# One copy of each RWKV chunk step to ScalarE, rope work held out of the lead-in, four affine values to VectorE

## The chip, the core and the metric

The kernel runs on one core of one Trainium2 chip. The engines are TensorE (PE in the profile, PEld for its weight loads), VectorE (DVE), ScalarE (ACT), GpSimd (POOL) and SyncE (SP), which here only issues DMAs. The metric is device time of one launch in microseconds, the median of several runs. Before the change it is 2287.57 us (three runs, 2287.49 to 2290.06).

## What is computed

Two layers of a hybrid decoder trunk over 1024 tokens of width 1024, then an RMSNorm. Cut to what matters here:

```python
mod = c_act @ w_ada + b_ada                      # shift, scale, gate
h = rms_norm(x, norm_g) * (1.0 + scale) + shift  # the affine values
proj = h @ w_in                                  # one wide projection
# three mixers on parts of proj: pooling, retention (rotary on q and k), RWKV-7
def step(S, inp):                                # RWKV-7, per head of 64
    r_t, w_t, k_t, v_t, a_t, b_t = inp
    sa = jnp.einsum('bhvk,bhk->bhv', S, a_t)
    S = (S * w_t[:, :, None, :] + sa[..., None] * b_t[:, :, None, :]
         + v_t[..., None] * k_t[:, :, None, :])
    return S, jnp.einsum('bhvk,bhk->bhv', S, r_t)
y = jnp.einsum('btnw,nwd->btnd', branches, w_branch)
merged = jnp.sum(sigmoid(gate_logits) * y, axis=2)
x = x + gate * (merged @ w_out)
```

## The kernel before

**How the order comes about.** The program is first recorded as a list of operations (class `Log`, from line 205), each with the operations it has to wait for, kept in `o.after`: value 1 means "after its end", value 2 "after its start". Then `plan` (line 334) replays the list with a cost model of each engine: at each step it takes the engine that can start soonest and gives it the ready operation with the smallest key. Only then are the instructions emitted, in that order, and each engine runs its own list strictly in order. All instructions are issued from line 540, so groups of the profile are told apart by the names of their tiles. A subtraction on GpSimd in some lanes may be planned on VectorE instead (`flex`). Because the plan is greedy and one list, an operation added or moved at one place shifts the order of nearly everything behind it.

**Number format of the big matmuls.** Every wide operand is split in a high and a low part, `hhi` and `hlo` for the activations, `wh` and `wl` (or `wbig`) for weights, and each product is the sum of three matmuls, hi by hi, lo by hi and hi by lo. The splits are a cast on ScalarE and a subtraction on GpSimd or VectorE.

**The lead-in** (`lead_in`, line 1810) is the first 70 or so microseconds. It loads x in two halves of 512 tokens (h) of eight tiles (kt), forms the RMSNorm, and forms shift and scale from `w_ada` in six groups: `coef(0)` to `coef(5)`; groups 4 and 5 give the coefficients of tiles 4, 5 and of tiles 6, 7. Each group, except group 1, is a chain of eight VectorE multiply-adds into `ada_ps`, the last into `ada_acc`, then tiny matmuls that sum over partitions (`sums`), then `mod` and `acoef` on VectorE (`ada_end`, line 736). Then `one(h, kt)` (line 1848) runs `affine` (line 1770): two ScalarE activations of the same values, one into `hhi`, one back into `x`; `low` subtracts to get `hlo`; `mms` multiplies with the first three weight items. `acc6` holds their six accumulators (`acc`, `ch`, `two`).

**Other work that the plan puts into the lead-in.** `setup_rest` (line 661) copies the constant `bone` and derives vectors of layer 1 (`omu`, `vec`) on VectorE. `rope_tables` (line 757), in lane "mix", makes sine and cosine for the retention's rotary, in two halves, from tiles `posi`, `ang`, `nrot`, `over`. They are recorded after the lead-in, but their inputs are there early, and `plan` places them where an engine is free in its model.

**The chunk step** (`rwkv_task`, lines 1514 to 1563). After preparation, each layer has four pairs of heads, each with 16 chunks of 64 tokens: 128 steps in all, each dependent on the one before. A step is: matmul `two<-S,AR`; VectorE adds to `xst`; two small matmuls `ch<-xst,G`, which solve the rows; a copy of the solved rows into `Z[0:64, c]` (line 1538, on VectorE); matmul `ch<-Z,BKt`; VectorE forms the next state `S`. Beside it ScalarE scales the state (`SP`) and copies the output (`y<-two`). TensorE fills the waits of a step with the big matmuls of projection items, as far as the plan foresees the waits; it leaves an estimated 300 ns of slack behind an operand from another engine.

**What follows.** Gates that are left, Strassen-like products of pairs of items (`forms`), the branch projections and the output projection, all big matmuls; and then the second layer.

Of the kernel before, what the change touches and what calls it, by code (L numbers as in the profile page):

```python
# [204 lines left out]
class Log:  # L205


    def __init__(self, nc, tc):
        self.nc, self.tc = nc, tc
        self.on = False  # L210
        self.ops = []
        self.tag = {}
        self.acc = {}
        self.lane = ""
        self.group = None
        self.real = {"DVE": nc.vector, "POOL": nc.gpsimd}
        self.vector = Proxy(self, "DVE", nc.vector)
        self.scalar = Proxy(self, "ACT", nc.scalar)
        self.gpsimd = Proxy(self, "POOL", nc.gpsimd)
        self.tensor = Proxy(self, "PE", nc.tensor)  # L220
        self.sync = Proxy(self, "SP", nc.sync)

    def call(self, eng, name, real, a, k):
        is_ap = lambda x: hasattr(x, "tensor") and hasattr(x, "ap")
        aps = [x for x in a if is_ap(x)] + [v for q, v in k.items() if q != "out" and is_ap(v)]
        if "out" in k:
            outs, ins = [k["out"]], aps
        else:
            outs, ins = aps[:1], aps[1:]
        o = self.group if self.on else None  # L230
        if isinstance(o, Op):
            o.calls.append((real, a, k, name))
            o.outs += outs
            o.ins_ += ins
        else:
            o = Op()
            o.eng, o.calls, o.outs, o.ins_ = eng, [(real, a, k, name)], list(outs), list(ins)
            o.lane, o.n, o.late, o.inst = self.lane, name, not self.on, None
            o.no_dep = o.own_dep = o.behind = None
            o.held = False  # L240
            o.flex = self.on and FLEX and eng == "POOL" and name == "tensor_tensor" and self.lane in FREE and k.get("op") != ALU.pow
            o.after, o.allocs, o.took = {}, [], []
            o.idx = len(self.ops)
            self.ops.append(o)
            if self.on and self.group is not None:
                self.group = o
        reads = ins + (outs if name == "matmul" and k.get("start") is False else [])
        for x, w in [(x, False) for x in reads] + [(x, True) for x in outs]:
            if x.space == DRAM and x.tensor.name.startswith(("in_", "out_t")):
                continue  # L250
            r = pieces(x)
            old = self.acc.setdefault(x.tensor.name, [])
            keep = []
            for p, pw, pr in old:
                if (w or pw) and p is not o and meet(r, pr):
                    o.after[p] = max(o.after.get(p, 0), 1)
                    if w and covers(r, pr):
                        continue
                keep.append((p, pw, pr))
            keep.append((o, w, r))  # L260
            self.acc[x.tensor.name] = keep
        if not self.on:
            o.inst = real(*a, **k)
        return o
# [289 lines left out]
def trunk_kernel(ctx, tc, xT, cvec, pos, vecs, consts, w_ada, w_all, pool_w, lora_w, out):  # L554
# [448 lines left out]
    def wprep(big=False):  # L1003
        if wready and wready[-1][0][0] == "forms":
            return
        for l, it in planner:
            if it[0] not in ("merge", "idle", "forms"):
                break
            wready.append((it, None))
            if it[0] != "merge":  # L1010
                return
        else:
            return
        t = None
        if it[0] == "out" and it[1] >= 2 and kept(l):
            if it[2]:
                wready.append((it, keep_w[it[1]]))
                return
            if it[1] < 6:
                t = r8("wout")  # L1020
            else:
                if it[1] == 6:
                    keep_w["G"] = gtile("wG")
                t = keep_w["G"][:, 2048 * (it[1] - 6) : 2048 * (it[1] - 5)]
        elif big:
            t = r8("wbig")
        parts = []
        for j in range(2):
            if t is not None:
                o = j * D  # L1030
                hi, lo = t[:, o : o + HF].bitcast(F32R), t[:, o + HF : o + D].bitcast(F32R)
            else:
                hi = wp.tile([P, HF], F32R, tag="wh", name=nm("wh"), bufs=3)
                lo = wp.tile([P, HF], F32R, tag="wl", name=nm("wl"), bufs=3)
            raw = wp.tile([P, HF], F32, tag="wr", name=nm("wr"), bufs=3)
            nc.sync.dma_start(out=raw, in_=w_all[l, ITEMS.index(it[:2] if it[0] == "out" else it), j])
            split(raw, hi, lo)
            parts.append((hi, lo))
        if it[0] == "out":
            keep_w[it[1]] = parts  # L1040
        wready.append((it, parts))
# [243 lines left out]
    def rwkv_task(l, hp, kT, rT, vp, lt, lw):  # L1285
# [228 lines left out]
        for c in range(16):  # L1514
            par = c % 2
            prog[(l, hp)] = c
            if c % 8 == 0:
                y = t_ri("y")
            S, Sn = SS[par], SS[1 - par]
            pcc = pc[:, c : c + 1]  # L1520
            SP = sb.tile([P, P], F32, tag="SP", name=nm("SP"), bufs=1)
            nc.scalar.activation(SP, S, AF.Copy, scale=pcc)
            cy = cyt()
            sa = mmul(cy[:, 0:P], jt(AR, slice(0, P), c), S)
            if c:
                sa.no_dep = yout[-1]
                sa.after[yout[-1]] = 2
            if c > 1:
                sa.own_dep = yout[-2]
            nc.vector.tensor_tensor(xst[0:64, :], cy[64:128, 0:P], AV[:, c * P : (c + 1) * P], op=ALU.add)  # L1530
            yield wait(xst)
            ch = ps_c.tile([P, HF], F32, tag="ch", name=nm("ch"))
            for hd in range(2):
                cols = slice(64 * hd, 64 * hd + 64)
                u0 = (16 * hd + c) * P
                n = min(65, 32 * P - u0 - 64)
                mmul(ch[0:n, cols], Gf[:, u0 + 64 : u0 + 64 + n], xst[:, cols])
            nc.vector.tensor_copy(Z[0:64, c, :], ch[0:64, 0:P])
            yield wait(Z)
            mmul(ch[:, P : 2 * P], BKt[:, c, :], Z[:, c, :])  # L1540
            for hd in range(2):
                rw = slice(64 * hd, 64 * hd + 64)
                nc.vector.scalar_tensor_tensor(
                    Sn[rw, rw], ch[rw, P + 64 * hd : P + 64 * hd + 64], pc[rw, c : c + 1], SP[rw, rw],
                    op0=ALU.mult, op1=ALU.add,
                )
            yield 500
            for hd in range(2):
                cols = slice(64 * hd, 64 * hd + 64)
                mmul(  # L1550
                    cy[0:65, cols],
                    G[:, 16 * hd + c, 0:65],
                    Z[:, c, cols],
                    start=False,
                    skip_group_check=True,
                )
            o = (c % 8) // 2 * P
            yout.append(nc.scalar.copy(y[64 * par : 64 * par + 64, o : o + P], cy[0:64, 0:P]).ins)
            yield wait(Sn)
            if c % 8 == 7:  # L1560
                h = c // 8
                yn = layer_norm(y, 8, 64, RWKV_EPS, t_ri, nc.gpsimd)
                posts[l, hp, h] = add("post", rwkv_post(l, hp, h, yn, bvs[h]))
# [206 lines left out]
    def affine(h, kt):  # L1770
        x = xin[h][kt]
        b, a = mod[0][:, SHIFT[kt] : SHIFT[kt] + 1], acoef[0][:, kt : kt + 1]
        hi, lo = hb("hhi"), hb("hlo")
        nc.scalar.activation(hi, x, AF.Identity, bias=b, scale=a)
        nc.scalar.activation(x, x, AF.Identity, bias=b, scale=a)
        h_cur[h].append((hi, lo))

    def low(eng, h, kt):
# [27 lines left out]
    def steps(g, n):  # L1806
        for _ in range(n):
            next(g)

    def lead_in():  # L1810
        V, G_ = nc.vector, nc.gpsimd
# [30 lines left out]
        def coef(g):  # L1842
            if g in COLUMNS:
                ada_columns(g)
            else:
                steps(gs[g], 9)

        def one(h, kt):
            normed(h, kt)
            affine(h, kt)  # L1850
            low(G_, h, kt)
            mms(h, kt)
# [33 lines left out]
        one(1, 3)  # L1886
        one(0, 5)
        coef(5)
        one(1, 4)
        one(0, 6)  # L1890
        one(1, 5)
# [15 lines left out]
    for i in range(3):  # L1907
        evac(FIRST[i], acc6[1][i], 1)
    wprep()
    setup_rest()  # L1910
    add("mix", rope_tables())
    late_ada = [(0, g) for g in (6, 7)] + [(1, g) for g in range(8)]

    for l in range(L):
# [468 lines left out]
```

## Time and profile before

| what | value |
|---|---|
| median of three runs | 2287.57 us |
| the profiled execution | 2284.81 us |
| its span | 2282.9 us |
| mean granted TensorE clock | 0.996 |
| VectorE busy | 1627.5 us (71%) |
| ScalarE busy | 907.4 us (40%) |
| GpSimd busy | 623.8 us (27%) |

Busy time is the sum of an engine's instructions. For TensorE it is rough: matmuls are pipelined, their ends are modelled, and a 128x512 one is shown as some 400 ns though the next starts some 230 ns later. A stall shorter than that difference does not show as idle time of PE; it does show before the weight load (PEld). "Who waited for whom" counts idle time of an engine before an instruction and names the operation that ended it.

### The profile page before, as it was taken

The page shows a single profiled execution, that of the slowest core. Times are in us where ns is not written, and L with a number is a line of the kernel's source. Part 1 is how long each engine was busy: PE and PEld are TensorE (multiplying, and loading weights), DVE is VectorE, ACT ScalarE, POOL GpSimd, SP SyncE. Part 2 cuts the span into 40 slices and gives each one's busy share as a digit, 9 for nine tenths or more (in the row PEclk, how much of TensorE's full clock was granted, in tenths as well). Part 3 has the DMA queues.
Part 4 walks back from the last instruction along what each step waited for, and adds up shares of the span by engine and source line. Part 5 has one row for each costly group of instructions (what it writes and reads, how often), then busy time and mean ns, then how long its engine had stood idle before and what let it go on. Part 6 is the DMA issues. An engine that isn't in the chain of part 4 may idle for free.

```text
span 2282.9 us, 35125 instructions
## 1 busy us (share of the span) xinstructions
PE 2246.9 (98%) x13076; PEld 1866.6 (82%) x13076; DVE 1627.5 (71%) x2907; ACT 907.4 (40%) x1671; POOL 623.8 (27%) x545
## 2 busy tenths in 40 slices
PE   7999999999999999999999999999999999999998
PEld 6788888888888888888888888888888888888888
DVE  7997876878888644667677778688785844465854
ACT  5734433434235344323454344243332444442243
POOL 2223323323325201331122232332432500041211
PEclk9999999999999999999999999999999999999999
DMA  8212111112356633664541111111122633256442
GB/s 317 81 49 67 33 44 47 44 50 76 117 165 210 213 126 97 226 191 164 170 131 34 41 33 39 56 39 47 51 71 75 194 116 111 88 171 225 133 131 84
DMA packets 138043, 248.86 MB, mean 109 GB/s; under 512 B 15632, under 2 KB 18960, under 8 KB 137872
## 3 DMA queue, kind: packets, MB, share of 16 engines
q1 hardware_dynamic: 137872, 246.61, 33.9%
q8 instruction: 103, 1.69, 0.3%
q14 instruction: 68, 0.56, 0.1%
HBM read 187.04 MB, written 59.51 MB: 108 GB/s over the span
## 4 chain that ended last, share of the span: by engine, by line
PE 89%; DVE 8%; issue 1%; ACT 1%; DMA 0%; POOL 0%; SPq 0%; DVEq 0%; POOLq 0%; ACTq 0%
PE acc L540 73%; PE two L540 3%; PE ch L540 3%; PE av L540 1%; PE ro L540 1%; PE g L540 1%; DVE two L540 1%; DVE tm L540 1%; DVE ksq L540 1%; PE lw L540 1%; PE m L540 1%; PE rkv L540 1%; PE bt L540 1%; DVE G L540 1%; PE rs L540 0%
## 5 line engine op out<-in xcount | busy, mean ns | idle before, releaser
L540 PE MATMUL acc<-hhi,wh 128*128 128x512 f32 x1488 | 599.3, 403 | 0.6 <-DVE vp L540 0.6
L540 PE MATMUL acc<-hlo,wh 128*128 128x512 f32 x1488 | 598.5, 402 | 0.0
L540 PE MATMUL acc<-hhi,wl 128*128 128x512 f32 x1488 | 595.9, 401 | 0.0
L540 POOL TENSOR_TENSOR wl<-wr,wh 128x512 fp32r<-128x512 f32 x175 | 237.9, 1361 | 582.2 <-ACT wh L540 485.3
L540 PEld LDWEIGHTS acc<-hhi,wh 128*128 128x128 f32 x1488 | 280.6, 189 | 51.2 <-issue 1.5
L540 PEld LDWEIGHTS acc<-hhi,wl 128*128 128x128 f32 x1488 | 280.7, 189 | 49.2 <-issue 0.7
L540 PEld LDWEIGHTS acc<-hlo,wh 128*128 128x128 f32 x1488 | 280.8, 189 | 48.6 <-issue 0.7
L540 ACT CAST wh<-wr 128x512 fp32r<-128x512 f32 x242 | 149.1, 617 | 292.8 <-PE acc L540 230.0
L540 PE MATMUL acc<-T,wh 128*128 128x512 f32 x576 | 177.5, 390 | 0.0
L540 PEld LDWEIGHTS acc<-T,wh 128*128 128x128 f32 x576 | 108.2, 188 | 22.4
L540 DVE TENSOR_TENSOR wl<-wsum,wh 128x512 fp32r<-128x512 f32 x75 | 53.5, 713 | 94.8 <-ACT wh L540 94.4
L540 ACT COPY y<-two 64x128 f32<-64x128 f32 x128 | 32.9, 257 | 211.7 <-PE two L540 208.2
L540 PE MATMUL acc<-T,wl 128*128 128x512 f32 x288 | 112.3, 390 | 0.0
L540 DVE SCALAR_TENSOR_TENSOR S<-ch,pc,SP 64x64 f32<-64x64 f32 x256 | 71.9, 281 | 54.8 <-PE ch L540 46.8
L540 POOL TENSOR_TENSOR oz<-ol,oz 128x512 fp32r<-128x512 f32 x10 | 14.3, 1435 | 327.9 <-DVE wl L540 259.2
L540 ACT CAST wh<-wsum 128x512 fp32r<-128x512 f32 x96 | 59.5, 620 | 95.8 <-PE acc L540 93.7
L540 DVE TENSOR_TENSOR xst<-two,MT 64x128 f32<-64x128 f32 x128 | 37.5, 293 | 68.9 <-PE two L540 44.9
L540 DVE TENSOR_TENSOR two<-two,tm 64x30 f32<-64x30 f32 (+14 forms) x240 | 78.8, 328 | 7.0
L540 DVE TENSOR_TENSOR tm<-MT,two 64x30 f32<-64x30 f32 (+14 forms) x240 | 76.3, 318 | 8.2 <-ACT two L540 1.3
L540 DVE TENSOR_TENSOR wl<-wraw,wh 128x512 fp32r<-128x512 f32 x53 | 37.6, 710 | 61.5 <-ACT wh L540 61.5
L540 PE MATMUL acc<-oy,wh 128*128 128x512 f32 x256 | 80.0, 394 | 0.0
L540 PE MATMUL acc<-oG,wh 128*128 128x512 f32 x256 | 79.0, 390 | 0.0
(328 smaller groups left out, 4899.6 us busy)
## 6 DMA issues: line engine op xcount, KB each, us to landing
wr<-in_w_all SPq DMA_DIRECT2D x268, 256.0 KB, 2.7
wraw<-in_w_all SPq DMA_DIRECT2D x96, 256.0 KB, 2.7
gd<-gsg SPq DMA_DIRECT2D x96, 256.0 KB, 2.0
gs<-gd SPq DMA_DIRECT2D x96, 256.0 KB, 3.8
wada<-in_w_ada SPq DMA_DIRECT2D x80, 256.0 KB, 3.1
ol<-od SPq DMA_DIRECT2D x48, 256.0 KB, 3.4
traw<-hd SPq DMA_DIRECT2D x32, 256.0 KB, 3.0
x<-in_xT SPq DMA_DIRECT2D x16, 256.0 KB, 5.1
```

Of the source, the lines that this page charges most:

```text
L540: o.inst = f(*a, **k)
```

## The change

Three edits. The copy of the solved rows in each chunk step goes from VectorE to ScalarE. Operations of `setup_rest` and `rope_tables` on VectorE, ScalarE and GpSimd get an added order, "not before the start of" the last operation of `coef(5)`; their DMAs, on SP, do not. And for tiles 6 and 7 the affine value that goes back into `x` is computed on VectorE; `hhi` stays on ScalarE.

```diff
@@ class Log
+        self.quiet = None
...
+            if self.quiet is not None and eng in ("DVE", "ACT", "POOL"):
+                o.after[self.quiet] = 2
@@ rwkv_task
-            nc.vector.tensor_copy(Z[0:64, c, :], ch[0:64, 0:P])
+            nc.scalar.copy(Z[0:64, c, :], ch[0:64, 0:P])
@@ affine
         nc.scalar.activation(hi, x, AF.Identity, bias=b, scale=a)
-        nc.scalar.activation(x, x, AF.Identity, bias=b, scale=a)
+        if kt < 6:
+            nc.scalar.activation(x, x, AF.Identity, bias=b, scale=a)
+        else:
+            nc.vector.tensor_scalar(x, x, a, b, op0=ALU.mult, op1=ALU.add)
@@ before lead_in
+    coefs = []
+
+    def quietly(gen):
+        while True:
+            nc.quiet = coefs[0]
+            dt = next(gen, None)
+            nc.quiet = None
+            if dt is None:
+                return
+            yield dt
@@ lead_in
         coef(5)
+        coefs.append(nc.ops[-1])
@@ after lead_in
+    nc.quiet = coefs[0]
     setup_rest()
-    add("mix", rope_tables())
+    nc.quiet = None
+    add("mix", quietly(rope_tables()))
```

## The prediction

> **What bounds the kernel now.** I read the page's busy line and chain first, then busy time by stretch, then who waited for whom.
>
> ```profile
> PE 2246.9 (98%) x13076; PEld 1866.6 (82%) x13076; DVE 1627.5 (71%) x2907; ACT 907.4 (40%) x1671; POOL 623.8 (27%) x545
> PE 89%; DVE 8%; issue 1%; ACT 1%; DMA 0%; POOL 0%; SPq 0%; DVEq 0%; POOLq 0%; ACTq 0%
> ```
>
> TensorE is busy for 98% of the span and makes 89% of the chain that ended last. The change removes no matmul. So it can win only where TensorE stands still or runs slowly. Busy time by stretch, in the order PE, PEld, DVE, ACT, POOL, and then the granted clock, says where that is:
>
> ```profile
> 0.00:100.00 100.00, 82.61 (x371) 68.01 (x371) 82.75 (x151) 63.98 (x102) 29.98 (x40) 0.95 0.62 218
> 100.00:2250.00 2150.00, 2139.59 (x12510) 1774.41 (x12510) 1532.61 (x2726) 834.78 (x1549) 591.04 (x502) 1.00 0.33 105
> PE acc L540 <- ACT hhi L540: 3.1, 3, 2.2
> PE acc L540 <- DVE hlo L540: 0.9, 1, 0.9
> PE ch L540 <- DVE Z L540: 2.7, 4, 1.2
> ```
>
> Of the first 100 us TensorE is idle for 17.4; of the next 2150 only for 10.4. The three waits shown are the ones that the edits can touch: two in the lead-in, one on the copied rows.
>
> **The change part by part.**
>
> *Rope and setup work leaves the lead-in.* This is the stretch with the 2.2 us wait: two windows around it and one before, and then the timeline of VectorE, ScalarE and TensorE (start, duration).
>
> ```profile
> 40.00:50.00 10.00, 8.63 (x37) 6.58 (x38) 9.03 (x19) 7.05 (x11) 7.13 (x7) 1.00 1.03 373
> 53.80:56.00 2.20, 0.00 (x0) 0.00 (x0) 2.20 (x6) 0.82 (x2) 0.00 (x0) 0.92 0.38 119
> 56.00:60.00 4.00, 3.99 (x11) 3.23 (x12) 3.93 (x8) 3.97 (x6) 1.29 (x1) 0.62 0.34 131
> ...
> 44.24 0.22 DVE L540 CAST bone<-braw 128x128 fp32r<-128x128 f32 x1
> ...
> 44.46 0.75 DVE L540 SCALAR_TENSOR_TENSOR ada_ps<-ringG,fixed,ada_ps 128x512 f32<-128x512 f32 x1
> ...
> 47.63 0.68 DVE L540 TENSOR_SCALAR vec<-vec 128x28 f32<-128x28 f32 x1
> 48.18 0.74 DVE L540 SCALAR_TENSOR_TENSOR ada_ps<-ringG,fixed,ada_ps 128x512 f32<-128x512 f32 x1
> 48.84 0.78 DVE L540 TENSOR_SCALAR vec<-vec 128x4 f32<-128x4 f32 x2
> 49.53 1.53 DVE L540 SCALAR_TENSOR_TENSOR ada_ps<-ringG,fixed,ada_ps 128x512 f32<-128x512 f32 x2
> 51.10 0.75 DVE L540 SCALAR_TENSOR_TENSOR ada_acc<-ringG,fixed,ada_ps 128x512 f32<-128x512 f32 x1
> ...
> 54.16 0.15 DVE L540 TENSOR_TENSOR mod<-sums,vec 128x4 f32<-128x4 f32 x1
> ...
> 54.95 0.15 DVE L540 SCALAR_TENSOR_TENSOR acoef<-mod,vec 128x2 f32<-128x2 f32 x1
> 55.14 0.81 ACT L540 ACTIVATE hhi<-x,mod,acoef 128x512 fp32r<-128x512 f32 x1 [2.28 <-DVE acoef L540]
> 56.01 2.92 PE L540 MATMUL acc<-hhi,wbig 128*128 128x512 f32 x6 [2.23 <-ACT hhi L540]
> ```
>
> The chain is `ada_ps`, `ada_acc`, `mod`, `acoef` of group 4, then `hhi`, then TensorE. VectorE is full, and foreign work stands inside the chain. By starts, bone and omu hold it for 44.46 - 44.24 = 0.22, the wide vec for 48.18 - 47.63 = 0.55, the small ones for 49.53 - 48.84 = 0.69: together 1.46 us. With them behind `coef(5)`, `acoef` comes 1.5 us earlier, and the gap of 2.2 shrinks to 0.7. The gain lies between nothing (the planner puts other work, such as a weight split, into the freed places) and the full 2.2; I take 1.5, which the rows give.
>
> Behind the gap the granted clock is 0.62 for 4 us: 0.38 x 4 = 1.5 us more. If the gap closes to 0.7, I expect the clock to stay up, since in 40 to 50 us, with 1.4 us of idle time in pieces, it is 1.00. Bounds nothing and 1.5; I take 1.5. [...]
>
> *Affine values of tiles 6 and 7.* Four activations leave ScalarE; four VectorE operations take their place. The row for such a one on VectorE is the scaling of the angles; the others show the last of the four before:
>
> ```profile
> L540 DVE TENSOR_SCALAR ang<-ang,cst x2: 480/481/482, 55.0 to 112.0; 128x512 f32<-128x512 f32 x2
> 74.08 1.28 ACT L540 ACT_TABLE_LOAD   x1
> 75.92 0.80 ACT L540 ACTIVATE x<-x,mod,acoef 128x512 f32<-128x512 f32 x1
> 77.49 0.50 PE L540 MATMUL acc<-hlo,wbig 128*128 128x512 f32 x1 [0.95 <-DVE hlo L540]
> 61.82 1.78 DVE L540 SCALAR_TENSOR_TENSOR ang<-nrot,ang 128x512 f32<-128x512 f32 x1
> 63.74 0.16 DVE L540 TENSOR_TENSOR mod<-sums,vec 128x4 f32<-128x4 f32 x1
> ```
>
> The last `x` stands in ScalarE's line behind a table load and evacuations, so `hlo` is late and TensorE waits 0.95 us. On VectorE it costs about 0.48, and nothing of that line is ahead of it. VectorE has the room, because rope work goes: the multiply-add of 1.78 us ahead of group 5's `mod` is one such piece. I take 0.95, bounds 0 and 0.95 (a POOL subtraction running beside it could stretch it, as it did that 1.78). Lead-in together: 1.5 + 1.5 + 0.95, about 4.0 (0 to 4.7).
>
> *Where the moved work lands.* From 44 to 64 us the foreign pieces are the 1.46 above, the 1.78, and four short rope steps of some 0.4 each: near 4.9 us of VectorE. No DMA moves. They now compete with the preparation of the first heads, where VectorE is full:
>
> ```profile
> 80.00:90.00 10.00, 10.00 (x46) 8.29 (x45) 9.97 (x15) 7.23 (x14) 0.41 (x2) 1.00 0.13 49
> ```
>
> PE is busy throughout, with projection items as cover; the lead-in ends 4 us earlier, so that the preparation ends about 1 us later against the clock of before. I charge 1.0; without the cover it is 4.9, at best 0.
>
> *The copy of the solved rows.* 128 copies. The rows: both engines' copies of that shape; the busy sum over the eight stretches in which steps run; how often each engine stood ready; what TensorE's weight load waited for; and one bad case.
>
> ```profile
> L540 DVE COPY Z<-ch 64x128 f32<-64x128 f32 x128 | 35.9, 280 | 33.4 <-PE ch L540 30.9
> L540 ACT COPY y<-two 64x128 f32<-64x128 f32 x128 | 32.9, 257 | 211.7 <-PE two L540 208.2
> sum 552.00, PE 546.43 PEld 454.64 DVE 380.37 ACT 195.42 POOL 165.71; mean PE 68.30 PEld 56.83 DVE 47.55 ACT 24.43 POOL 20.71
> DVE Z L540 <- PE ch L540: 30.9, 42, 1.0
> ACT y L540 <- PE two L540: 208.2, 106, 4.0
> PEld ch L540 <- DVE Z L540: 12.9, 31, 1.6
> PEld g L540 <- ACT BKt L540: 2.9, 8, 0.4
> L540 ACT COPY BKt<-bt 128x512 f32<-128x512 f32 x32 | 18.1, 586 | 12.4 <-PE bt L540 12.4
> ...
> 1721.44 1.75 DVE L540 SCALAR_TENSOR_TENSOR pd<-pt,pu 128x512 f32<-128x512 f32 x1 [0.82 <-POOL pt L540]
> 1723.22 0.28 DVE L540 COPY Z<-ch 64x128 f32<-64x128 f32 x1
> ...
> 1723.55 0.30 PEld L540 LDWEIGHTS ch<-Z,BKt 128*128 128x128 f32 x2 [1.62 <-DVE Z L540]
> ```
>
> The copy itself is no dearer on ScalarE (257 against 280 ns). What counts is what stands ahead of it. In the steps VectorE is busy 380 of 552 us, ScalarE 195. VectorE stood waiting for the solve in 42 of 128 cases; in 86 it was still at something else, and in the worst that was a 1.75 us operation, which left TensorE standing 1.62 us. The weight loads waited 12.9 us for `Z`: the most that can be won. ScalarE stood ready for its own copy of that shape in 106 of 128. If lateness follows that, 12.9 x 22/86 = 3.3 us are left and 9.6 won. By the other row, `BKt`, ScalarE costs 2.9/32 = 0.09 us per copy, 11.6 over 128, and 1.3 are won. I take the middle, 5.5. Below nothing the bound is a ScalarE that is always behind a cast; it is priced as a rival. [...] Queued behind the moved copy on ScalarE are the weight casts and `y`; none of them is waited for at once.
>
> **The sum.** 4.0 - 1.0 + 5.5 = 8.5 us less: the profiled 2284.81 (span 2282.9 and 1.9 around it) becomes 2276.3. The median lies 2.8 above the profiled run, so the forecast on the median is 2287.57 - 8.5 = 2279.1. The plan is made anew from 44 us on; TensorE's other idle time after 100 us is 10.4 - 2.7 = 7.7, and I allow half of it, 4 us, either way.
>
> **The rivals.**
> - *Stalls move with the copy.* The step's wait becomes one on ScalarE and only the lead-in pays: -4.0 + 1.0 = -3.0, 2284.6. For it: the planner leaves the same slack for either engine, and the `BKt` row. Against: 106 of 128.
> - *The lead-in does not get shorter,* so that the edit does not do what it says: the freed places go to weight splits, the gap stays. Then -0.95 + 1.0 - 5.5, about 2282.1. For it: the plan is greedy. Against: the pieces are plain in the chain.
> - *The clock still dips,* with the gap closed: 8.5 - 1.5 = 7.0, 2280.6. [...]
> - *Everything pays in full:* 4.7 + 12.9 = 17.6 less, 2270.0.
> - *Slower: ScalarE's order holds the steps.* It runs in order and carries casts of 617 ns:
>
> ```profile
> L540 ACT CAST wh<-wr 128x512 fp32r<-128x512 f32 x242 | 149.1, 617 | 292.8 <-PE acc L540 230.0
> ```
>
>   Such a cast often waits itself, for TensorE to free a slot; a `Z` copy behind it stops TensorE's next step. Break-even: 12.9 of old stalls plus 3.0 of lead-in, over 128 steps, is 0.12 us a step; beyond 0.16 it is slower by more than 0.2%. At half a cast, 0.31 us for each, the stalls are 39.7, and the time 2287.57 - 3.0 + 26.8 = 2311.4; at 0.2 it is 2297.3. Against it: ScalarE is idle 65% of these stretches.
>
> **How the numbers follow.** A measurement of this kernel can tell about 0.2%, 4.6 us: faster means below 2283.0, slower above 2292.1. Chances: forecast 0.34; clock dips 0.08; all in full 0.08; lead-in not shorter 0.14; stalls move 0.25; slower 0.11. Forecast, clock and full are faster (0.50), of "lead-in not shorter" about 0.09, of "stalls move" 0.01: 0.60. Same gets the rest, 0.29. The range 2270.5 to 2289.0 takes in all but the last rival and half of the full one.
>
> **What would show it.** Right: no TensorE gap over 1 us between 45 and 60 us and a clock near 1.00 there; no `bone`, `vec`, `ang` on VectorE before group 5's `acoef`; no wait on `hlo` at the end of the lead-in; TensorE's first evacuations some 4 us earlier; weight loads waiting for ACT `Z` under 8 us in place of 12.9. Wrong: a wait for `hhi` as long as before, waits on ACT `Z` above 13 us, new waits on VectorE between 70 and 170 us, or other waits after 100 us grown by more than 4 us.

## The result and the profile after

| | median | runs | profiled execution | its span |
|---|---|---|---|---|
| before | 2287.53 us | 4 (2285.1 to 2290.06) | 2284.81 us | 2282.9 us |
| after | 2277.22 us | 4 (2276.13 to 2278.98) | 2278.98 us | 2277.1 us |

The changed kernel takes 0.9955 of the time of before (95% interval 0.9943 to 0.9968), 10.3 us less on the medians. The two profiled executions differ by only 5.8 us, since that of before lies 2.7 us below its median and that of after 1.8 above; sums over the two traces have to be held against the 5.8. In the changed kernel all instructions are issued from line 543.

The busy line of the page, then busy time by stretch (PE, PEld, DVE, ACT, POOL, granted clock), of after:

```profile
PE 2247.6 (99%) x13076; PEld 1868.1 (82%) x13076; DVE 1610.0 (71%) x2793; ACT 934.0 (41%) x1795; POOL 609.6 (27%) x535
...
0.00:100.00 100.00, 86.14 (x383) 71.26 (x384) 82.20 (x151) 62.06 (x100) 28.50 (x37) 0.98 0.63 218
100.00:2250.00 2150.00, 2142.48 (x12546) 1778.44 (x12545) 1519.32 (x2622) 864.84 (x1680) 579.11 (x496) 1.00 0.33 105
...
56.00:60.00 4.00, 3.96 (x11) 3.12 (x12) 3.50 (x6) 3.94 (x6) 0.00 (x0) 0.63 0.34 131
```

The matmuls are the same 13076. Behind 100 us TensorE is idle for 7.5 us in place of 10.4. Between 56 and 60 us its clock still dips, to a mean of 0.63, as it did before (0.62). The 86.14 busy us of the first 100, 82.61 before, are only in part a gain; the last section shows why.

**Who waited for whom behind 100 us.** First two rows of before that the prediction did not need, then the rows of after: what the weight loads of a chunk step waited for, and how often ScalarE stood ready for the copy (us in total, times, longest).

```profile
PEld ch L540 <- DVE xst L540: 5.6, 17, 0.5
PEld two L540 <- DVE S L540: 1.4, 6, 0.3
```

```profile
PEld two L543 <- DVE S L543: 6.5, 16, 0.8
PEld ch L543 <- DVE xst L543: 5.4, 17, 0.5
PEld g L543 <- ACT BKt L543: 4.1, 12, 0.4
PEld ch L543 <- ACT Z L543: 1.4, 3, 0.6
...
ACT Z L543 <- PE ch L543: 122.8, 103, 2.6
```

Two things are to be seen. The wait for the copied rows is almost gone, 1.4 us in place of 12.9: ScalarE stood ready for the solve in 103 of 128 steps, where VectorE did in 42. And part of it came back one operation later: the next step's weight load waits 6.5 us for the state `S`, 1.4 before, and `BKt` costs 4.1 in place of 2.9. The four together were 12.9 + 1.4 + 2.9 + 5.6 = 22.8 and are 17.4. That these 5.4 us come close to the 5.8 between the two profiled executions is in part chance: some of them returned at other operands, since all idle time of weight loads from 100 to 2250 us together fell by 4.2 us, from 64.3 to 60.1.

**The lead-in.** Three more rows of the timeline of before, then those of after (start, duration):

```profile
43.45 0.15 DVE L540 TENSOR_TENSOR mod<-sums,vec 128x2 f32<-128x2 f32 x1
...
52.83 0.95 PE L540 MATMUL sums<-fixed,ada_acc 128*128 128x1 f32 x8
...
70.24 0.69 ACT L540 ACTIVATE lt<-acc,vec 128x511 f32<-128x511 f32 x1
```

```profile
44.44 0.15 DVE L543 TENSOR_TENSOR mod<-sums,vec 128x2 f32<-128x2 f32 x1
...
45.66 0.68 DVE L543 TENSOR_TENSOR hlo<-x,hhi 128x512 fp32r<-128x512 f32 x1
...
51.69 0.75 DVE L543 SCALAR_TENSOR_TENSOR ada_acc<-ringG,fixed,ada_ps 128x512 f32<-128x512 f32 x1
...
53.80 0.95 PE L543 MATMUL sums<-fixed,ada_acc 128*128 128x1 f32 x8
...
54.78 0.16 DVE L543 TENSOR_TENSOR mod<-sums,vec 128x4 f32<-128x4 f32 x1
54.98 0.16 DVE L543 SCALAR_TENSOR_TENSOR acoef<-mod,vec 128x2 f32<-128x2 f32 x1
...
56.04 2.09 PE L543 MATMUL acc<-hhi,wbig 128*128 128x512 f32 x6 [1.30 <-ACT hhi L543]
...
62.35 1.77 DVE L543 TENSOR_TENSOR wbig<-wr,wbig 128x512 fp32r<-128x512 f32 x1
...
70.75 0.69 ACT L543 ACTIVATE lt<-acc,vec 128x511 f32<-128x511 f32 x1 [1.46 <-PE acc L543]
```

Both kernels issue the same instructions in the same order up to about 44 us, yet after is already 44.44 - 43.45 = 0.99 us late there, so distances from group 3's `mod` are compared. To group 4's `acoef` it was 54.95 - 43.45 = 11.50 us and is 54.98 - 44.44 = 10.54. To the first evacuation (`lt`, the first read of the accumulators) it was 26.79 and is 26.31. Setup and rope work did leave: `bone` comes at 65.21, behind group 5's `acoef`. But an `hlo` subtraction (0.60 to the start of what follows it) now stands in the freed places at 45.66, and a split of `wbig` of 1.77 us stands ahead of group 5's `mod`, where a rope step of 1.78 stood. TensorE's gap ahead of `hhi` is 1.30 us.

### The profile page after: what moved, and what is told of

The parts are those of the page before. It is cut to its first block, busy times and chain, and to the rows that moved or that the text cites. A ratio compares the mean times of both kernels' runs of the same rounds, so it can differ in the third digit from the quotient of the medians.

```text
span 2277.1 us, 35068 instructions
## 1 busy us (share of the span) xinstructions
PE 2247.6 (99%) x13076; PEld 1868.1 (82%) x13076; DVE 1610.0 (71%) x2793; ACT 934.0 (41%) x1795; POOL 609.6 (27%) x535
## 4 chain that ended last, share of the span: by engine, by line
PE 65%; DVE 3%; issue 1%; ACT 0%; POOL 0%; DVEq 0%; POOLq 0%; ACTq 0%
PE acc L543 57%; PE two L543 2%; PE ch L543 1%; PE g L543 1%; PE av L543 1%; PE ro L543 0%; DVE two L543 0%; DVE tm L543 0%; DVE ksq L543 0%; PE m L543 0%; DVE G L543 0%; PE lw L543 0%; PE bt L543 0%; PE rs L543 0%; PE ssps L543 0%
## 5 line engine op out<-in xcount | busy, mean ns | idle before, releaser
L543 POOL TENSOR_TENSOR wl<-wr,wh 128x512 fp32r<-128x512 f32 x168 | 229.1, 1365 | 581.2 <-ACT wh L543 418.4
L543 ACT CAST wh<-wsum 128x512 fp32r<-128x512 f32 x96 | 59.5, 620 | 90.8 <-PE acc L543 85.5
L543 ACT COPY Z<-ch 64x128 f32<-64x128 f32 x128 | 33.0, 258 | 123.0 <-PE ch L543 122.8
```

Of the source, the lines that this page charges most:

```text
L543: o.inst = f(*a, **k)
```

## The experiments

Each kernel was timed beside before on the same chip. Edit 1 is the moved copy, edit 2 the order "not before the last of `coef(5)`", edit 3 the affine values on VectorE.

| kernel | edits | median | ratio to before, 95% interval |
|---|---|---|---|
| z_only | 1 | 2279.64 us | 0.9965 (0.9953 to 0.9978) |
| quiet_only | 2 | 2292.08 us | 1.0019 (1.0010 to 1.0028) |
| aff_only | 3 | 2299.16 us | 1.0051 (1.0037 to 1.0065) |
| no_z | 2, 3 | 2288.62 us | 1.0004 (0.9995 to 1.0013) |
| z_quiet | 1, 2 | 2280.86 us | 0.9972 (0.9960 to 0.9983) |
| after_again | 1, 2, 3 | 2278.39 us | 0.9959 (0.9947 to 0.9972) |
| swap_exec | order of before, copy on ScalarE | 2280.77 us | 0.9973 (0.9964 to 0.9982) |
| swap_plan | order of after, copy on VectorE | 2302.35 us | 1.0066 (1.0054 to 1.0079) |
| z_margin | before, more slack behind the copy | 2296.31 us | 1.0040 (1.0028 to 1.0053) |
| replan_b1 | before, slack 310 ns everywhere | 2285.77 us | 0.9992 (0.9983 to 1.0001) |
| replan_a1 | after, slack 310 ns everywhere | 2281.17 us | 0.9969 (0.9958 to 0.9979) |
| noflex | after, splits of the lead-in kept on GpSimd | 2282.99 us | 0.9983 (0.9974 to 0.9992) |

**Which edit carries the gain.** Edit 1 alone, in the kernel before:

```diff
-            nc.vector.tensor_copy(Z[0:64, c, :], ch[0:64, 0:P])
+            nc.scalar.copy(Z[0:64, c, :], ch[0:64, 0:P])
```

> The kernel before with the first edit alone: the copy of the solved rows on ScalarE. If the gain comes from the moved copy (the trace of after is behind that of before until 600 us, and its gains lie at 600 to 700 and 1350 to 1700 us, where chunk steps run): 2278 to 2281. By the prediction's own terms (5.5 of 8.5 in the steps): 2282. If the lead-in carried the gain: 2286 to 2288. If it is only the luck of a new order: anywhere from 2280 to 2290, with no link to the weight loads' wait for Z.

It takes 8.3 us off the median (2287.93 to 2279.64, before measured beside it), and 5.0 off the span of the profiled execution. What the weight loads of a step waited for in it:

```profile
PEld ch L540 <- DVE xst L540: 5.9, 17, 0.6
PEld g L540 <- ACT BKt L540: 4.3, 12, 0.4
PEld two L540 <- DVE S L540: 4.1, 13, 0.8
PEld ch L540 <- ACT Z L540: 0.8, 2, 0.4
```

The four make 15.1, 7.7 less than the 22.8 of before. `Z` gives 12.1, and `S`, `BKt` and `xst` take back 2.7 + 1.4 + 0.3. All idle time of weight loads behind 100 us fell by 4.8 us, from 64.3 to 59.5, so some 3 of the 7.7 returned at other operands. The 4.8 are close to the 5.0 between the two spans; a trace shows one execution and not the 8.3 between the medians.

The other two edits without the first (no_z; the diff is against after):

```diff
-            nc.scalar.copy(Z[0:64, c, :], ch[0:64, 0:P])
+            nc.vector.tensor_copy(Z[0:64, c, :], ch[0:64, 0:P])
```

> The kernel after with the first edit undone: the copy on VectorE, rope and setup work held back, the last affine values on VectorE. If the moved copy carries the gain: 2285 to 2288, weight loads waiting some 13 us for Z again. By the prediction's terms (4.0 - 1.0 in the lead-in): 2284.5. If the lead-in carried all: 2277 to 2280.

Nothing is won: 0.7 us above before, and the interval, 1.1 us faster to 3.0 slower, leaves out the 3.0 us of gain that the prediction gave these edits. Where the held-back work went is seen in one stretch of before, then in the same of no_z, with the wait for the copy in the whole run, and last in the same stretch of after:

```profile
180.00:200.00 20.00, 20.00 (x125) 16.92 (x125) 11.99 (x32) 10.10 (x22) 9.27 (x9) 1.00 0.37 112
```

```profile
180.00:200.00 20.00, 19.06 (x111) 14.87 (x110) 16.45 (x37) 10.49 (x20) 9.22 (x8) 1.00 0.29 75
...
PEld ch L543 <- DVE Z L543: 14.8, 32, 1.6
```

```profile
180.00:200.00 20.00, 19.50 (x116) 15.54 (x115) 17.25 (x33) 11.01 (x25) 10.09 (x9) 1.00 0.36 98
```

In the first chunk steps of no_z VectorE is busy for 16.45 of 20 us in place of 11.99, with rope's `ang` and `nrot` between the copies, TensorE starts 111 matmuls in place of 125, and the wait for `Z` in the whole run grows from 12.9 to 14.8. So what the lead-in gained is lost there again. After pays in the same stretch too, though its copy is on ScalarE: 116 matmuls in place of 125. The time of no_z lies 0.6 us above the range that was expected with the gain in the copy.

Edit 2 and edit 3, each alone in the kernel before (their hunks as in the change):

> The kernel before with the second edit alone: rope and setup work held behind the coefficients of tiles 6 and 7. The two lead-in edits together gave 2288.6 against 2287.9. If the rope work that was held back lands on VectorE in the first chunk steps (168 to 193 us in that trace) and makes their copies late, this alone is 2287 to 2290, with the loss there. If the affine edit was what spoiled it: 2283 to 2285.

> The kernel before with the third edit alone: the last four affine values on VectorE. By the prediction's term: 0.95 less, 2287.0. If VectorE, full in the lead-in, delays its other work for it: 2288 to 2290. Either way the wait on hlo near 77 us goes.

Both are slower, by 4.1 and by 11.2 us on the medians, and both lie above every range that was expected. For four operations of half a microsecond 11.2 us is out of proportion, so it can hardly be their own cost. The stretch in which layer 0's chunk steps end, of before and of aff_only, and one matmul's wait in the latter:

```profile
690.00:720.00 30.00, 30.00 (x135) 24.82 (x135) 24.77 (x30) 16.97 (x31) 21.03 (x15) 1.00 0.66 218
```

```profile
690.00:720.00 30.00, 25.01 (x129) 18.57 (x128) 25.59 (x42) 15.39 (x31) 18.26 (x15) 0.98 0.62 196
...
716.95 0.66 PE L540 MATMUL yt<-cst,yc 128*128 128x128 f32 x4 [3.28 <-POOL yc L540]
```

Here TensorE loses 5.0 us, 3.28 of them in one wait for an output normalization on GpSimd, 650 us behind the edit. No matmul of the new order covers it. Why the order lost its cover there was not followed up, nor where the rest of the 11.2 us went, nor where edit 2 alone loses.

**Is it the engine, or the new order?** Edit 1 also makes the plan anew. In swap_exec the plan of before is kept on every engine, and only the 128 copies are issued on ScalarE, at the place in its line that they come to in the order of the plan; swap_plan does the reverse with the plan of after.

```diff
-                o.inst = f(*a, **k)
+                o.inst = (o.swap or f)(*a, **k)
...
-            nc.vector.tensor_copy(Z[0:64, c, :], ch[0:64, 0:P])
+            z_ = nc.vector.tensor_copy(Z[0:64, c, :], ch[0:64, 0:P])
+            z_.swap = nc.nc.scalar.copy
```

> The order planned for the kernel before, kept for every engine; only when it is emitted do the 128 copies go to ScalarE, at the place in time that they had on VectorE. No new plan, nothing else changed. If the gain is that ScalarE is not late where VectorE was (stretched or queued operations ahead of the copy): the weight loads' wait for Z falls from 12.9 to under 5 us and the time by 4 to 8, to 2280 to 2283. If the gain comes from the new order: 2286 to 2289, and waits elsewhere take the place of those on Z.

> The order planned for the kernel after, kept for every engine; only when it is emitted do the 128 copies go to VectorE. If the gain is ScalarE's punctuality in the steps: waits on Z come back (10 us or more) and the time is 2283 to 2288. If the new order carries it: 2277 to 2280 still.

The engine alone is worth 7.2 us (4.1 to 8.2 by the interval). In swap_exec:

```profile
PEld ch L540 <- ACT Z L540: 5.5, 12, 1.9
PEld g L540 <- ACT BKt L540: 2.9, 8, 0.4
PEld two L540 <- DVE S L540: 0.3, 1, 0.3
```

The wait for `Z` falls by 7.4 us, to a little over the 5 that were expected; `BKt` does not rise, and `S` falls by 1.1. The move also takes the 35.9 us of the copies off VectorE, so some of the gain may be that its other work comes earlier; the rows put 7.4 us on `Z` and 1.1 on `S`. In swap_plan the order of after meets the copy on VectorE, and the time is 2302.35, some 25 us above after and 14 above what was expected:

```profile
PEld ch L543 <- DVE Z L543: 34.6, 61, 1.6
```

So the order of after is worth nothing without the move. It was made for a VectorE without the 128 copies, so this does not say how punctual VectorE is in an order made for it. That its stretched two-input operations, like the 1.75 us one that the prediction shows (the 16 of that form in before have a median of 0.69), are why 300 ns of slack were too little there is argued and not shown.

**Would more slack have done it on VectorE?** z_margin leaves 500 in place of 300 ns behind this copy alone:

```diff
-                    gap += MARGIN
+                    gap += o.swap or MARGIN
...
+            z_.swap = 500
```

> The kernel before, the copy on VectorE, but the plan leaves 500 in place of 300 ns between the estimated end of that copy and TensorE's use of it. If what costs is TensorE standing still because the copy is later than the plan thinks, and the length of a step is hidden by projection work: the waits on Z fall to 6 us or less and the time by 3 to 7, to 2281 to 2285, though every step gets 0.2 us longer (26 us over 128). If steps bound the time: 2290 and up. If VectorE's load was the cost in another way: 2287 to 2289.

The wait for `Z` falls to 3.1 us, as was expected, and still the kernel is 8.4 us slower than before, as expected if steps bound the time. The steps do end later: the last copy of layer 0 starts at 700.4 us in place of 688.9, that of layer 1 at 1821.4 in place of 1774.7. Where they end, TensorE stands still, in layer 0 at the same place as in aff_only, and again in layer 1:

```profile
PEld ch L540 <- DVE Z L540: 3.1, 11, 0.8
...
700.00:710.00 10.00, 6.02 (x24) 3.69 (x22) 9.70 (x15) 7.79 (x15) 6.90 (x7) 0.81 0.70 208
...
707.82 0.80 PE L540 MATMUL acc<-hhi,wh 128*128 128x512 f32 x1 [3.58 <-ACT wh L540]
...
1829.72 0.80 PE L540 MATMUL acc<-hhi,wh 128*128 128x512 f32 x1 [3.50 <-ACT wh L540]
```

Of 700 to 710 us 4.0 are idle, at a clock of 0.81, and another wait of 2.43 us for `yc` follows, where before had no idle time at all. A likely reading is that longer steps used up the matmuls that were cover here before; that is argued and not shown, and it is not told apart from the steps simply ending too late. Whether slack could win with these two places mended was not tried.

**How much is the luck of an order?** Two controls change the slack of everything by 10 ns, which shifts the order and means nothing else:

```diff
-MARGIN = 300
+MARGIN = 310
```

> The kernel before with the plan's general slack at 310 in place of 300 ns, a change of no meaning in itself, to see what a new order alone does. If the effects above are more than the luck of an order: 2285 to 2291, waits on Z still 10 to 16 us.

> The changed kernel with the planner's slack at 310 in place of 300 ns, nothing else: another order with the same edits. Theory A (the gain belongs to the copy on ScalarE and holds in a new order): 2274 to 2282 us, ratio below 0.9975. Rival B (the gain is one lucky order): above 2283.

Before moves by 2.2 us, with an interval that takes in no change; after stays 7.2 us below before, where it had 10.0 beside it. The gain lives in a new order, and some 2 or 3 us of any difference here may be the order's.

**What edits 2 and 3 add to edit 1.**

> The changed kernel as it is, beside the two variants of it below. Theory A (edit 1 alone carries the gain; edits 2 and 3 give nothing by themselves and at most a little with it): 2277 to 2280 us, ratio 0.9950 to 0.9970, not told apart from the run with edit 1 alone (2279.64). Rival B (edits 2 and 3 add 2.4 us or more once the copy stands on ScalarE): 2276 to 2277.5, ratio 0.9955 or below.

> Edits 1 and 2, with all affine values on ScalarE as before. Theory A (the affine edit is worth the 0.95 us of the hlo wait at most): that wait of about 0.9 is back, and the time is within 1.5 us of the changed kernel. Rival B (the affine edit matters by the order that it gives to the rest, as it did alone, where it cost 11 us): more than 3 us from the changed kernel, on either side, with the difference behind 100 us and not in the lead-in.

After is 10.0 us below before, edits 1 and 2 are 7.5, edit 1 alone (in another set of runs) was 8.3. After_again and z_quiet were measured in one set, and no run of the one reaches the other (2276.78 to 2279.01 against 2279.61 to 2282.32), so the 2.5 us between these two kernels are real. They lie between what theory A and rival B allowed, and whether they belong to edit 3 or to the order is not settled, since a meaningless shift moves 2 or 3 us. The wait for `hlo` that theory A wanted back in z_quiet did not come back: in its order the last `x` activation stands ahead of the table load and the evacuations on ScalarE, where in before it stood behind them. That detail was wrong.

**Would the freed places have paid if the splits had stayed away?** noflex forbids the move to VectorE for the splits recorded in the lead-in from behind `one(0, 2)` to `one(1, 7)`:

```diff
-            ... and k.get("op") != ALU.pow
+            ... and k.get("op") != ALU.pow and not self.stay
```

> The changed kernel, where the subtractions of the lead-in's hlo and wbig recorded after one(0, 2) stay on GpSimd and may not be planned on VectorE. Theory A (the places that rope work left were filled by these splits, so that group 5's coefficients and the gap before hhi gained little): group 4's acoef comes 0.7 us or more earlier than 54.98, group 5's mod no longer has 1.77 us of a split ahead of it, the first evacuation comes 1 to 2 us earlier and the time is 1 to 2 us below the changed kernel. Rival B (the splits are needed on VectorE, because GpSimd alone is too slow for them): waits of TensorE for hlo or wbig appear in the first 75 us, and the time is 1 to 6 us above the changed kernel.

What theory A expected did not come. The time is 4.6 us above after, and group 4's `acoef`, at 54.83 us, came 10.67 us behind group 3's `mod`, where after has 10.54. The timeline of noflex, first the lead-in, then a place in the first chunk steps:

```profile
50.82 0.75 DVE L544 SCALAR_TENSOR_TENSOR ada_acc<-ringG,fixed,ada_ps 128x512 f32<-128x512 f32 x1
...
52.39 2.34 DVE L544 SCALAR_TENSOR_TENSOR ada_ps<-wada,fixed,ada_ps 128x512 f32<-128x512 f32 x3
54.64 0.15 DVE L544 TENSOR_TENSOR mod<-sums,vec 128x4 f32<-128x4 f32 x1
...
62.48 1.77 DVE L544 TENSOR_TENSOR wl<-wr,wh 128x512 fp32r<-128x512 f32 x1
...
198.76 1.28 ACT L544 ACT_TABLE_LOAD   x1
...
200.71 0.63 ACT L544 ACTIVATE nrot<-ang 64x512 f32<-64x512 f32 x1
...
201.35 1.28 ACT L544 ACT_TABLE_LOAD   x1
202.65 0.60 ACT L544 ACTIVATE silu<-acc 128x512 f32<-128x512 f32 x1
...
204.10 0.30 PEld L544 LDWEIGHTS ch<-Z,BKt 128*128 128x128 f32 x2 [3.01 <-ACT Z L544]
```

In the lead-in `ada_acc` did come early, and TensorE summed it from 51.97 on; but three multiply-adds of group 5 stood ahead of `mod` on VectorE, until 54.64. And the place ahead of group 5's `mod` did not become free: a split of `wl`, which the edit leaves movable, took 1.77 us there. So the run does not tell what a lead-in without splits on VectorE would be worth. Some 3 of the 4.6 us are a single wait at 204 us: rope's two sine activations (the second is shown), with a table load on either side, stand on ScalarE ahead of a `Z` copy. That is the prediction's slower rival, at one place of 128. The rival of noflex was right on the time and wrong on the place: no wait for `hlo` or `wbig` grew. A table load takes 1.28 us in these rows, and they show nothing more beside it: `silu` starts 1.30 us after the load begins, which itself begins as `nrot` ends.

No version was faster than after; edit 1 alone, with one changed line, gives 8.3 us where all three give 10.0 to 10.3, each beside its own measurement of before.

## Why the prediction was right, and which of its terms were not

The forecast was 2279.1, with 8.5 us less than before; 10.3 were measured, and the range held. The direction and the largest term, the copy, were right by their mechanism. That the sum came so close is luck: the lead-in's term was too large and the copy's too small.

- **The lead-in, 4.0 us: wrong.** By the waits it gave 1.9: the gap ahead of `hhi` fell by 0.93, from 2.23 to 1.30, and the `hlo` wait of 0.95 went. Edits 2 and 3 without edit 1 left none of it in the time, where 3.0 were forecast after the 1.0 of moved work. The step that failed is "With them behind `coef(5)`, `acoef` comes 1.5 us earlier, and the gap of 2.2 shrinks to 0.7". It came 0.96 earlier, mostly for other reasons than the three pieces. On VectorE itself, from `mod` of group 3 to the end of `ada_acc`, 8.40 us became 8.00 and not 6.94, because an `hlo` took 0.60 of the freed places, as the rival "the lead-in does not get shorter" had it, and group 3's `acoef`, now beside a GpSimd subtraction, held VectorE for 0.50 in place of 0.06. The chain then left VectorE: `ada_acc` was ready at 51.85 in before, and TensorE's line got to `sums` only at 52.83, in after at 52.44 and 53.80. Time won ahead of `ada_acc` only lengthened that wait, by 0.38. The rest came behind it: 0.35 between the start of `sums` and `mod`, and 0.59 between `mod` and `acoef`, where one of group 5's multiply-adds no longer stands. The rows for this were in the trace of before: `sums` started 0.98 us after its operand, behind other matmuls.
- **The clock, 1.5 us of it: wrong.** The clock stood at 0.50 for 3.4 us before and for 3.4 us after, so nothing was won; the rival "the clock still dips" was right. The premise, a gap of 0.7, was not met, so no run shows what such a gap would do. But the reading under it, that the gap lowers the clock by its length, does not hold either: the clock of after fell 1.0 us behind the end of its gap (last section).
- **The `hlo` wait, 0.95: gone, but edit 3 was not needed for it,** since it was gone in z_quiet too. There TensorE waits elsewhere, 0.68 us for `pu` at 95 us and 0.53 for `lw` at 83, and its first evacuation comes 26.83 us behind group 3's `mod`, in after 26.31. Three of the four new `x` operations took 0.54 to 0.55 us on VectorE, the fourth 1.62 us beside a GpSimd subtraction of 1.60, a stretch that the prediction allowed for.
- **The moved work, 1.0: at least 1.9 where the copy is on VectorE** (the wait for `Z`, 12.9 to 14.8 in no_z). Where it is on ScalarE it still costs something: in 180 to 200 us of after TensorE is idle for 0.50 us, in before for none, and starts 9 matmuls fewer. This fits a reading in which edit 1 makes edit 2 less harmful; it is not measured apart.
- **The copy, 5.5 us: right in its mechanism, too small.** 7.2 by the engine alone, 8.3 with its plan. The row of readiness was the better guide: ScalarE stood ready in 103 of 128 steps, and the wait fell by 11.5 to 12.1, more than the 9.6 that it gave. What the prediction did not have is that 4 to 6 us come back on `S` and `BKt` in a plan that knows of ScalarE, and none in swap_exec, which keeps the old plan; that the fill moves up to the next tight operand is the likely reading, not shown. By the prediction's own signs the 5.1 us on `S` in after are one of being wrong, a wait grown by more than 4. The rival "stalls move" expected them on ScalarE; there only `BKt` grew, by 1.2.
- **The slower rival** did not occur: the wait for ACT `Z` is 1.4 us, not 39.7. Its mechanism is real, as noflex shows at one step.
- **The plan made anew, allowed 4 us either way: too narrow for single edits** (11.2 for aff_only), about right for the whole.

## What to carry to other kernels

Here a small copy on the chain of a serial step was better off on the engine that is most often ready when its input arrives; count that in the rows of who waited for whom, and then look for the operand that is tight next, since a part of the gain went there. Before you price work that leaves a chain, follow the chain over every engine: if the next engine's line starts late by its own order, time won ahead of it is not won. And where a planner orders everything, run an edit alone and in a shifted order, because the plan's own luck is worth as much as a small edit.

## What the runs showed of the hardware that was not expected

The 0.99 us that after is late at 44 us, with the same instructions, comes from TensorE's rate. Before, then after, by timeline and by stretch:

```profile
25.04 2.73 PE L540 MATMUL sums<-fixed,ringG 128*128 128x1 f32 x24
29.82 1.44 PE L540 MATMUL sums<-fixed,sq 128*128 128x1 f32 x6 [2.04 <-DVE mod L540]
...
28.25:28.50 0.25, 0.00 (x0) 0.00 (x0) 0.25 (x1) 0.00 (x0) 0.00 (x0) 0.67 1.05 385
55.50:55.75 0.25, 0.00 (x0) 0.00 (x0) 0.25 (x2) 0.25 (x1) 0.00 (x0) 0.78 0.82 311
```

```profile
25.06 5.11 PE L543 MATMUL sums<-fixed,ringG 128*128 128x1 f32 x24
30.43 1.44 PE L543 MATMUL sums<-fixed,sq 128*128 128x1 f32 x6 [0.25 <-DVE mod L543]
...
28.00:30.00 2.00, 2.00 (x11) 2.00 (x10) 1.61 (x4) 0.00 (x0) 0.00 (x0) 1.00 1.05 384
57.00:57.25 0.25, 0.25 (x3) 0.20 (x2) 0.25 (x1) 0.25 (x1) 0.00 (x0) 0.65 0.00 0
```

The same 24 matmuls took 2.73 us in one run and 5.11 in the other, 0.11 and 0.21 us each, with the clock shown as 1.00 for the slow ones. In before TensorE ran them at the faster rate from about 25 us, ran out of work at 27.8 and waited 2.04 us; 0.5 us into that wait its clock fell to 0.50. In after it ran them at the slower rate and waited only 0.25 us behind them. So a fuller first 100 us was no gain by itself here, and a clock of 1.00 ahead of the first dip stood beside either rate. The order does not explain it: swap_exec, with the order of before, had group 3's `mod` at 44.10, 0.65 us later than before. Its 24 matmuls had begun 0.45 us earlier than in before (24.59), so from there to `mod` it lost 1.10 us.

In these two traces the clock does not follow the single gaps. Read in stretches of 0.25 us, it fell in before at 28.3 us (0.67 in that stretch), rose at 35.2 (0.68), fell at 55.6 (0.78) and rose at 59.1 (0.89), which is 2, 6 and 1 times 3.41 us apart; in after it fell at 57.1 (0.65) and rose at 60.5 (0.53), 3.41 us later. The three falls came 0.5 us into the wait of 2.04 us, 1.9 us into the gap of 2.23, and 1.0 us behind the end of the gap of 1.30; 24, 8 and 8 matmuls of 128x1 stand ahead of these gaps. None of the three stretches of 3.41 us that ended in a fall was idle throughout: TensorE ran the 24 and the 8 small matmuls in the first two, and in the one that ended at 57.1 us it stood still for 1.30 us and ran 128x512 matmuls for the last 1.0. What sets the time of a fall or a rise is not shown.
